# A hybrid decoder layer on one core: decay with a bias in the exponential, splits on VectorE, tables in pieces, and new planner costs

## The chip, the cores and the metric

The kernel runs on one core of a Trainium2 chip. The metric is the device time of one execution in microseconds (us). The engines are TensorE (PE; its weight loads are PEld), VectorE (DVE), ScalarE (ACT), GpSimd (POOL) and SyncE (SP), whose queue issues most of the DMAs. Each engine runs its own instructions in order and waits on semaphores for the others.

## What is computed

One decoder layer over 2048 tokens of width 1024, all in float32: a normalised input goes through one projection, three groups of heads read parts of it, their outputs are gated, projected and added to the input, and a last normalisation follows.

```python
h = rms_norm(x, norm_in)
c_q, c_kv, k_rope, gdn_qkv, gdn_a, gdn_b, mem_q, gate = split_cols(h @ w_in, IN_SPLITS)
...
qkv = silu(causal_depthwise_conv(gdn_qkv, gdn_conv))
gq, gk = l2_normalize(gq), l2_normalize(gk)
beta = sigmoid(gdn_b); g = -exp(a_log) * softplus(gdn_a + dt_bias)
...
g = cumsum(g, axis=-1)
decay = exp(where(incl, g[..., :, None] - g[..., None, :], -inf))
L = where(strict, einsum(k_beta, k) * decay, 0)
T = triangular_solve(L + eye, eye)
...
mixed = concatenate([o_mla, o_gdn, o_mem]) * silu(gate)
y = rms_norm(x + mixed @ w_out, norm_final)
```

The three groups have four heads each: causal attention with low-rank queries and keys and rotary positions (MLA), a gated delta rule (GDN), and attention over 256 memory tokens.

## The kernel before

**Stages.** The tokens are worked on in two halves of 1024, each as two blocks of 512. The input projection streams 34 column tiles of `w_in` (`stream`, `run_unit`) over the resident, transposed input. Beside it run, for each half, four GDN heads (`delta_head`), the two low-rank paths (`low_rank` with `q_use` and `kv_use`), and once the projection of the memory tokens (`mem_proj`). Then come the attention scores and values, and last the output projection with the final norm (`out_half`).

**Precision.** A float32 product is made of three passes of a faster type: an operand is split into a rounded part (`hh`, `wh`) and the rest (`hl`, `wl`), and `mm3` multiplies hi by hi, hi by lo and lo by hi into one PSUM tile (`ip` for the input projection). For every half tile of weights `w_split` makes `wh` (a copy, on ACT or DVE by `copy`) and `wl` (a subtraction, on POOL or DVE by `lesser`). `small_weights` does the same for the low-rank and memory weights (`bwh`, `bwl`).

**A GDN head.** After convolution and normalisation, `delta_head` loads rows of the cumulated decay to all partitions (`gr`), subtracts the column's own value (line 903), adds a mask (904), and takes the exponential on ACT (905). The score blocks (`kk`) times this decay give `LT`, which goes through DRAM (`lsys`, `lt`) to POOL. POOL solves 32x32 triangular systems in 62 small `TENSOR_TENSOR` instructions (`pr`, `X`; lines 949 to 955), and the result returns through DRAM (`tsys`) into `inv`. DVE transposes its blocks (`STREAM_TRANSPOSE mid<-inv`), PE joins them (`inv` matmuls), and a scan over eight chunks follows, in which each step waits for the one before: PE (`pa`), DVE (`r`), PE, ACT (`vn`), PE, DVE (the new state, `st` and `st_odd` in turn), PE. At every fourth chunk transposed values `vt` and keys `kt` are scaled from PSUM on DVE (line 1028).

**Rotary positions.** `trig_tables` writes sine and cosine to DRAM (`trig`). `key_rope` loads each table twice into 64 partitions, `q_use` four times into 128, by `trig_load`: one DMA whose source has a leading broadcast dimension of 2 or 4. `key_rope` runs four times and `q_use` loads four times, so there are eight `cs` and eight `sn` loads.

**What sets the order.** The program is written out by a planner in Python. It keeps a clock per engine (`T`), adds to it the cost of each instruction as it is recorded (`act_cost`, `dve_cost`, `pool_cost`, `pe_cost`), and lets the foreground (the projection, later attention) run until a background generator is due by that clock. A `yield n` in a generator says how many ns to wait after its last step. Several constants take part: `CBIAS` in `copy` chooses ACT or DVE, `SLACK` and the POOL clock in `lesser` choose POOL or DVE, `BACK` says how far ahead of PE's clock a DMA may be issued, `MEM_AT` after how many tiles of a half `mem_proj` starts. So every cost and constant moves the places of instructions on all engines. Nearly all instructions pass through one recording helper and carry its line, 259; they are told apart by their tiles.

Of the kernel before, what the change touches and what calls it, by code (L numbers as in the profile page):

```python
# [15 lines left out]
ALU = mybir.AluOpType  # L16
# [19 lines left out]
EARLY = 0.0  # L36
BACK = 2000.0
AVM = 600.0
SECOND = 2
TRIG_AT = 1  # L40
MEM_AT = 44
STRICT = False
SPARE = 500.0
LONG = "012k3q", "0123qk"
CONV = 4
CBIAS = 2000.0
DEFER = -1500.0
# [20 lines left out]
def hybrid_layer(ctx, tc, a, out):  # L68
# [154 lines left out]
    def pool_cost(op, args, kw, out):  # L223
        if op == "tensor_tensor":
            return 147 + 2.1 * free(out)
        fast = op == "tensor_scalar" and kw["op0"] == ALU.mult and kw.get("op1") == ALU.add
        return 160 + (0.85 if fast or op == "memset" else 3.4) * free(out)

    def pe_cost(op, args, kw, out):
        src = args[2] if op == "matmul" else args[1]  # L230
        if op == "transpose":
            return 109 if src.shape[0] > 32 else 53
        n, m, k = free(src), free(args[1]), src.shape[0]
        if src.dtype == F32:
            return 1.667 * max(n, m) + 4 if n >= 96 or k < P else 3.33 * max(n, m)
        return 0.4167 * n + 3

# [292 lines left out]
    def trig_load(t, i, c, n):  # L530

        dma(out=t[0:n * 32],
            in_=trig[i, c].unsqueeze(0).broadcast_to([n, 32, 512]))

# [79 lines left out]
    def w_split(w):  # L614
        wh = sb.tile([P, 512], F32R, name="wh", tag="wh", bufs=3)
        copy(wh, w)
        wl = sb.tile([P, 512], F32R, name="wl", tag="wl", bufs=3)
        lesser("wl").tensor_tensor(wl, w, wh, op=ALU.subtract)
        return wh, wl
# [131 lines left out]
    def token_scalars(hf, res):  # L751
# [6 lines left out]

        at, bt, z, z2, pl, gc = (tk(i) for i in range(6))
        dma(out=at, in_=ab[hf, 0:4].rearrange("h (c t) -> (h c) t", t=P))  # L760
        dma(out=bt, in_=ab[hf, 4:8].rearrange("h (c t) -> (h c) t", t=P))
        yield 3500

# [32 lines left out]
        V.scalar_tensor_tensor(ce, eg, -1.0, bt, op0=ALU.mult, op1=ALU.mult)  # L796
        V.tensor_scalar(hb, bt, 0.5, None, op0=ALU.mult)
        dma(out=rows_g[hf].rearrange("(r t) -> r t", t=P), in_=gc)
        dma(out=rows_l[hf].rearrange("(r t) -> r t", t=1), in_=eg[:, P - 1:P])
# [4 lines left out]
        pc = psg("pc")  # L804
        for i, t in enumerate((gc, hb, ce, rem, eg)):
            PE.transpose(pc[:, i * 32:(i + 1) * 32], t, ident[0:32, 0:32])
# [36 lines left out]
    def delta_head(hf, h, q, k, res):  # L843
# [53 lines left out]
        for b in range(2):  # L897
# [4 lines left out]
            gr3 = gr.rearrange("p (c t) -> p c t", t=P)  # L902
            V.tensor_tensor(gr3, gr3, gc.unsqueeze(2).broadcast_to([P, 4, P]), op=ALU.subtract)
            V.tensor_tensor(gr3, gr3, neg.unsqueeze(1).broadcast_to([P, 4, P]), op=ALU.add)
            A.activation(gr, gr, AF.Exp)
            k3, q3 = (t[:, bs].rearrange("p (c t) -> p c t", t=P) for t in (k, q))
# [111 lines left out]
        for c in range(NCK):  # L1018
            cl = h * 8 + c
            if c % 4 == 0:  # L1020
# [3 lines left out]
                for src, o, dst, col in ((v, 0, vt, cols[:, 1, cl:cl + 4]), (k, c, kt, kfac[:, 1, c:c + 4])):  # L1024
                    ps = psg("tr")
                    for cc in range(4):
                        PE.transpose(ps[:, cc * P:(cc + 1) * P], src[:, (o + cc) * P:(o + cc + 1) * P], ident)
                    V.tensor_tensor(dst, ps.rearrange("p (c t) -> p c t", t=P),
                                    col.unsqueeze(2).broadcast_to([P, 4, P]), op=ALU.mult)
                    yield 0  # L1030
# [61 lines left out]
    def small_weights(srcs):  # L1092
# [6 lines left out]
        def split(w):  # L1099
# [3 lines left out]
            wl = sb.tile([P, n], F32R, name="bwl", tag="m2", bufs=9)  # L1103
            lesser("bwl").tensor_tensor(wl, w, wh, op=ALU.subtract)
            return wh, wl
# [645 lines left out]
    def out_half(tb, n, ps, ss):  # L1751
# [4 lines left out]
        yield 0  # L1756
        A.activation(xo[:, 1, ns], xo[:, 0, ns], AF.Square, accum_out=ss[:, n:n + 1])
        if n == 0:
            return
# [4 lines left out]
        V.reciprocal(rs, rs)  # L1764
        yield 0
        for n in range(2):
            ns = slice(n * 512, (n + 1) * 512)
# [432 lines left out]
```

## Time and profile before

| | |
|---|---|
| median of three runs | 1797.79 us (1794.03 to 1803.4) |
| the profiled execution | 1803.16 us, its span 1801.3 us |
| PE busy | 1741.0 us, 97% of the span |
| DVE, ACT, POOL busy | 65%, 41%, 28% |
| mean granted TensorE clock | 0.987 |

The profile is of one execution. A row of the timeline has start and duration in us, engine, operation, the tiles written and read, shapes, and in brackets how long the engine was idle before it and what released it. In windows, "busy (x)" is busy time with the number of instructions, PEclk the granted TensorE clock as a share of full speed, DMA the mean busy share of the 16 DMA engines. A PE busy share near 100% says only that no gap is seen, since matmuls are pipelined; their number in a window tells the pace.

### The profile page before, as it was taken

To read this page: it belongs to the slowest core of one execution; us is meant where nothing else is said; L and a number is where in the kernel's file an instruction comes from. 1 tells how busy PE (TensorE), PEld (TensorE's weight loads), DVE (VectorE), ACT (ScalarE), POOL (GpSimd) and SP (SyncE) were. 2 spreads that over 40 slices of the span, in tenths; PEclk is the share of its full clock that TensorE was granted. 3 is DMA by queue.
4 is the path that set the end of the run, shared out by engine and by line. 5 is a ranking of instruction groups with operands and counts; after the bars stand their busy time and mean duration, and the time that the engine had idled before them with its cause. 6 is when DMAs were issued, how large, how long until landed. Compare 5 with 4: busy or idle time off the path is not lost.

```text
span 1801.3 us, 28573 instructions
## 1 busy us (share of the span) xinstructions
PE 1741.0 (97%) x9776; PEld 1466.0 (81%) x9776; DVE 1170.3 (65%) x2629; ACT 732.4 (41%) x1880; POOL 500.4 (28%) x891
## 2 busy tenths in 40 slices
PE   7999999999999999999999999999999999999998
PEld 6778787888877787887888787899999998888886
DVE  7877766776686847666556754777776777345343
ACT  7444233342453535253334432446465556212121
POOL 1421743351631124434432261001011012321120
PEclk9999999999999999999999998999999999999999
DMA  7544474436556343576633567835342536666551
GB/s 269 163 129 147 140 231 126 144 113 211 157 181 209 111 152 115 173 225 199 205 121 103 174 183 229 254 117 153 87 157 66 157 113 197 197 188 185 165 169 49
DMA packets 225826, 291.19 MB, mean 162 GB/s; under 512 B 30320, under 2 KB 130672, under 8 KB 225680
## 3 DMA queue, kind: packets, MB, share of 16 engines
q1 hardware_dynamic: 218640, 273.62, 48.8%
q0 software_dynamic: 7040, 15.74, 3.1%
q8 instruction: 77, 1.26, 0.3%
q14 instruction: 69, 0.57, 0.1%
HBM read 197.79 MB, written 91.49 MB: 161 GB/s over the span
## 4 chain that ended last, share of the span: by engine, by line
PE 45%; DMA 3%; DVE 2%; POOL 2%; issue 1%; ACT 0%; SPq 0%; DVEq 0%; POOLq 0%; ACTq 0%
PE op L259 15%; PE sc L259 10%; PE av L259 7%; PE ip L259 5%; PE pt L259 4%; PE pa L259 1%; POOL X L259 1%; PE qb L259 1%; POOL pr L259 1%; DMA sn<-trig 1%; PE mk L259 1%; PE mv L259 0%; PE inv L259 0%; SPq L305 0%; DMA og<-gatem 0%
## 5 line engine op out<-in xcount | busy, mean ns | idle before, releaser
L259 PE MATMUL ip<-hh,wh 128*128 128x512 f32 x1088 | 457.6, 421 | 10.8 <-ACT hh L259 8.2
L259 PE MATMUL ip<-hh,wl 128*128 128x512 f32 x1088 | 432.5, 398 | 4.9 <-DVE wl L259 4.1
L259 PE MATMUL ip<-hl,wh 128*128 128x512 f32 x1088 | 432.2, 397 | 0.0
L259 PEld LDWEIGHTS ip<-hh,wl 128*128 128x128 f32 x1088 | 207.3, 191 | 50.7 <-DVE wl L259 4.5
L259 PEld LDWEIGHTS ip<-hh,wh 128*128 128x128 f32 x1088 | 208.5, 192 | 47.2 <-ACT hh L259 8.2
L259 PEld LDWEIGHTS ip<-hl,wh 128*128 128x128 f32 x1088 | 208.7, 192 | 34.8 <-DVE hl L259 0.5
L259 POOL TENSOR_TENSOR wl<-wr,wh 128x512 fp32r<-128x512 f32 x73 | 105.8, 1449 | 408.3 <-ACT wh L259 357.4
L259 ACT CAST wh<-wr 128x512 fp32r<-128x512 f32 x143 | 88.5, 619 | 170.3 <-PE ip L259 115.3
L259 DVE TENSOR_TENSOR tl<-pt,th 128x512 fp32r<-128x512 f32 (+2 forms) x208 | 119.7, 584 | 28.0 <-ACT th L259 25.9
L259 DVE SCALAR_TENSOR_TENSOR y<-raw,gdn_conv,y 128x512 f32<-128x512 f32 x144 | 118.1, 824 | 23.0 <-ACT y L259 21.4
L259 PE MATMUL sc<-kn,qn 128*128 128x512 f32 (+2 forms) x480 | 132.7, 380 | 0.4 <-DMA qn<-qn 0.4
L259 PE MATMUL op<-wop,mh 128*128 128x512 f32 x416 | 130.8, 395 | 0.0
L259 PE MATMUL av<-th,vn 128*128 128x256 f32 x576 | 130.8, 288 | 0.0
L259 ACT CAST th<-pt 128x512 fp32r<-128x512 f32 (+2 forms) x157 | 80.3, 517 | 101.3 <-PE pt L259 92.0
L259 POOL TENSOR_TENSOR pr<-X,lt 128x60 f32<-128x60 f32 (+24 forms) x248 | 97.7, 394 | 58.9 <-DMA lt<-lsys 40.1
L294 POOL DMA_DIRECT2D mix<-mo x64 | 34.8, 544 | 263.4 <-ACT mo L259 179.7
L259 PEld LDWEIGHTS av<-th,vn 128*128 128x128 f32 x576 | 99.3, 190 | 4.7 <-ACT th L259 0.7
L259 POOL TENSOR_TENSOR X<-X,pr 128x60 f32<-128x60 f32 (+24 forms) x248 | 96.6, 390 | 19.4
L259 PE MATMUL sc<-kr,qr 128*128 128x512 f32 (+2 forms) x320 | 97.9, 383 | 0.0
L259 PEld LDWEIGHTS op<-wop,mh 128*128 128x128 f32 x416 | 77.4, 188 | 17.7
L259 ACT ACTIVATE s<-s,m 128x768 f32<-128x768 f32 (+13 forms) x71 | 79.1, 1115 | 30.3 <-DVE mx L259 30.3
L259 POOL TENSOR_TENSOR og<-og,orow 128x512 f32<-128x512 f32 x28 | 40.9, 1485 | 171.9 <-DMA orow<-ri 117.0
(285 smaller groups left out, 3581.9 us busy)
## 6 DMA issues: line engine op xcount, KB each, us to landing
wr<-in_w_in SPq DMA_DIRECT2D x148, 256.0 KB, 3.0
fr<-rows_n SPq DMA_DIRECT2D x48, 256.0 KB, 4.6
mxo<-mix SPq DMA_DIRECT2D x16, 768.0 KB, 5.4
craw<-craw SPq DMA_DIRECT2D x40, 256.0 KB, 2.8
x<-in_xT SPq DMA_DIRECT2D x32, 256.0 KB, 5.2
gatem<-gt SPq DMA_DIRECT2D x32, 256.0 KB, 2.9
qn<-qn SPq DMA_DIRECT2D x32, 256.0 KB, 3.3
kn<-kn SPq DMA_DIRECT2D x32, 256.0 KB, 3.0
```

The lines of the kernel that those rows point to most:

```text
L259: return pinned(f(*args, **kw))
L294: pinned(nc.gpsimd.dma_start(out=raw(out), in_=raw(in_)))
```

## The change

1. `token_scalars` also makes the negated cumulated decay `ngc`, and its column form takes the place of `gc` in `cols`. In `delta_head` the subtraction on DVE is gone; the exponential is four ACT instructions of 128 columns, each with its column of `ngc` as bias.
2. `kt` is written by four ACT instructions with the column factor as scale; `vt` stays on DVE.
3. `trig_load` issues one DMA per copy of the table, each into 32 partitions.
4. `wl` and `bwl` are always made on DVE.
5. For the last token block, `out_half` multiplies by the gain before the row's factor is known, scales the halves on ACT and DVE, and stores them in two DMAs.
6. The planner's costs and constants: a POOL `tensor_tensor` costs more (290 + 2.25 per column for 147 + 2.1), a matmul costs 5 ns more, `BACK` 4000 for 2000, `MEM_AT` 30 for 44, `CBIAS` 500 for 2000, and `token_scalars` waits 2000 for 3500.

```diff
-BACK = 2000.0
+BACK = 4000.0
-MEM_AT = 44
+MEM_AT = 30
-CBIAS = 2000.0
+CBIAS = 500.0
@@ pool_cost, pe_cost
-            return 147 + 2.1 * free(out)
+            return 290 + 2.25 * free(out)
-        return 0.4167 * n + 3
+        return 0.4167 * n + 8
@@ trig_load
-        dma(out=t[0:n * 32],
-            in_=trig[i, c].unsqueeze(0).broadcast_to([n, 32, 512]))
+        for j in range(n):
+            dma(out=t[j * 32:(j + 1) * 32], in_=trig[i, c])
@@ w_split (and bwl in small_weights)
-        lesser("wl").tensor_tensor(wl, w, wh, op=ALU.subtract)
+        V.tensor_tensor(wl, w, wh, op=ALU.subtract)
@@ token_scalars
-        yield 3500
+        yield 2000
+        V.tensor_scalar(ngc, gc, -1.0, None, op0=ALU.mult)
-        for i, t in enumerate((gc, hb, ce, rem, eg)):
+        for i, t in enumerate((ngc, hb, ce, rem, eg)):
@@ delta_head
-            V.tensor_tensor(gr3, gr3, gc.unsqueeze(2).broadcast_to([P, 4, P]), op=ALU.subtract)
             V.tensor_tensor(gr3, gr3, neg.unsqueeze(1).broadcast_to([P, 4, P]), op=ALU.add)
-            A.activation(gr, gr, AF.Exp)
+            for c in range(4):
+                A.activation(gr3[:, c, :], gr3[:, c, :], AF.Exp, bias=gc[:, c:c + 1])
-                    V.tensor_tensor(dst, ps.rearrange("p (c t) -> p c t", t=P),
-                                    col.unsqueeze(2).broadcast_to([P, 4, P]), op=ALU.mult)
+                    if dst is kt:
+                        for cc in range(4):
+                            A.activation(kt[:, cc, :], ps[:, cc * P:(cc + 1) * P], AF.Copy, scale=col[:, cc:cc + 1])
+                    else:
+                        V.tensor_tensor(dst, ps.rearrange("p (c t) -> p c t", t=P),
+                                        col.unsqueeze(2).broadcast_to([P, 4, P]), op=ALU.mult)
@@ out_half, last token block
+        ends = tb == out_order()[-1]
+        if ends:
+            V.tensor_tensor(xo[:, 0, ns], xo[:, 0, ns], gf[0][:, ns], op=ALU.mult)
...
+        if ends:
+            A.activation(xo[:, 0, 0:512], xo[:, 0, 0:512], AF.Copy, scale=rs)
+            dma(out=out[tb * P:(tb + 1) * P, 0:512], in_=xo[:, 0, 0:512])
+            V.tensor_scalar(xo[:, 0, 512:1024], xo[:, 0, 512:1024], rs, None, op0=ALU.mult)
+            dma(out=out[tb * P:(tb + 1) * P, 512:1024], in_=xo[:, 0, 512:1024])
+            give(hb=1)
+            return
```

By count, DVE gets 73 `wl` of the streamed weights that POOL had (75 become 148), 19 `bwl`, and 42 copies to `wh` and `bwh` that ACT had (`wh` 5 become 41); it loses 16 `gr` subtractions and 16 `kt`. POOL keeps the solves, the table arithmetic and the output stage. SP's queue gets 33 DMAs more.

**DVE at the second head's inversion** (`mid<-inv` are its block transposes, `st` and `st_odd` the first head's scan). Before:

```order
L259 SCALAR_TENSOR_TENSOR r<-pa,kfac,vt 128x128
L259 SCALAR_TENSOR_TENSOR y<-raw,gdn_conv,y 128x512
L259 SCALAR_TENSOR_TENSOR y<-raw,y 128x512
L259 TENSOR_TENSOR elo<-vb,ehi 128x512
L259 STREAM_TRANSPOSE mid<-inv_280 32x256 x2
L259 SCALAR_TENSOR_TENSOR st_odd<-st_253,el,pa 128x128
L259 SCALAR_TENSOR_TENSOR r<-pa,kfac,vt 128x128
```

and in the changed kernel:

```order
L259 TENSOR_TENSOR y<-y,fr 128x512
L259 TENSOR_TENSOR gr<-gr,norms 128x512
L259 SCALAR_TENSOR_TENSOR gt<-th,gt 128x512
L259 TENSOR_TENSOR wl<-wr,wh 128x512
L259 STREAM_TRANSPOSE mid<-inv_280 32x256
L259 SCALAR_TENSOR_TENSOR st_253<-st_odd,el,pa 128x128
L259 STREAM_TRANSPOSE mid<-inv_280 32x256
L259 TENSOR_TENSOR vt<-tr,cols 128x512
```

A state update still stands behind a transpose. On PE, the order puts 331 matmuls between this head's last `kk` and its first `inv` before, and 359 in the changed kernel.

**DVE at the third rotary table load of the queries** (`ra`, `rb`, `rc` read the tables `cs` and `sn`). Before:

```order
L259 SCALAR_TENSOR_TENSOR r<-pa,kfac,vt 128x128
L259 RECIPROCAL ri_259<-sm 128x1
L259 TENSOR_TENSOR ra<-qb,cs 128x512
L259 TENSOR_TENSOR rb<-qb,sn 128x512
L259 TENSOR_TENSOR rc<-qb,cs 128x512
L259 SCALAR_TENSOR_TENSOR st_odd<-st_256,el,pa 128x128
```

and in the changed kernel:

```order
L259 TENSOR_TENSOR ra<-qb,cs 128x512
L259 TENSOR_TENSOR rb<-qb,sn 128x512
L259 TENSOR_TENSOR rc<-qb,cs 128x512
L259 TENSOR_TENSOR vt<-tr,cols 128x512
L259 TENSOR_TENSOR cs<-qb,sn 128x512
L259 TENSOR_TENSOR ra<-ra,rb 128x512
L259 TENSOR_TENSOR rc<-rc,cs 128x512
L259 SCALAR_TENSOR_TENSOR r<-pa,kfac,vt 128x128
```

The rotation now stands ahead of the head's first scan step instead of inside it.

**DVE at the first head's decay** (`wl` needs the `wh` of its half tile). Before:

```order
L259 TENSOR_TENSOR gr<-gr,cols 128x512
L259 TENSOR_TENSOR sn<-ra,cs 64x512
L259 TENSOR_TENSOR gr<-gr,neg 128x512
L259 SCALAR_TENSOR_TENSOR y<-raw,gdn_conv,y 128x512
L259 TENSOR_TENSOR kq<-y,fr 128x4x128
L259 SCALAR_TENSOR_TENSOR y<-raw,gdn_conv,y 128x512
L259 TENSOR_TENSOR raw<-ip,rms 128x512
L259 TENSOR_TENSOR wl<-wr,wh 128x512
```

and in the changed kernel, behind the same decay rows:

```order
L259 TENSOR_TENSOR sn<-ra,cs 64x512
L259 SCALAR_TENSOR_TENSOR y<-raw,y 128x512
L259 TENSOR_TENSOR raw<-ip,rms 128x512
L259 CAST wh<-wr 128x512
L259 SCALAR_TENSOR_TENSOR y<-raw,gdn_conv,y 128x512
L259 TENSOR_TENSOR wl<-wr,wh 128x512
L259 SCALAR_TENSOR_TENSOR y<-raw,gdn_conv,y 128x512 x2
L259 TENSOR_TENSOR wl<-wr,wh 128x512
```

The subtraction `gr<-gr,cols` is gone; two splits now stand within seven rows of DVE's queue, one of them with its copy.

## Rows read from the trace of the kernel before

**Rows 1.** The page: busy time, share of the span and instructions of each engine.
```profile
PE 1741.0 (97%) x9776; PEld 1466.0 (81%) x9776; DVE 1170.3 (65%) x2629; ACT 732.4 (41%) x1880; POOL 500.4 (28%) x891
```

**Rows 2.** Windows of PE, output stage: window, PE busy (x), PEclk, DMA share, GB/s.
```profile
1575.00:1620.00 45.00, 45.00 (x198) 1.00 0.64 195
```

**Rows 3.** Windows, input stage: PE, PEld, DVE, ACT, POOL busy (x), PEclk, DMA, GB/s.
```profile
0.00:270.00 270.00, 249.05 (x1191) 202.11 (x1192) 197.24 (x405) 118.96 (x277) 103.40 (x171) 0.97 0.58 180
0.00:1110.00 1110.00, 1064.13 (x5795) 874.81 (x5796) 748.24 (x1526) 450.09 (x1210) 399.31 (x728) 0.98 0.54 168
```

**Rows 4.** Waits of PE: who waited for whom, us in total, times, longest.
```profile
PE pa L259 <- DVE st_odd L259: 12.6, 7, 3.5
...
PE ip L259 <- DVE wl L259: 4.1, 1, 4.1
...
PE pc L259 <- DVE tks L259: 2.4, 2, 2.3
...
PE inv L259 <- DVE mid L259: 1.0, 2, 0.6
```

**Rows 5.** Windows at PEclk 0.50; columns as in Rows 3.
```profile
71.90:75.30 3.40, 3.00 (x8) 2.30 (x8) 1.02 (x1) 0.67 (x3) 3.15 (x4) 0.50 1.26 70
133.40:140.10 6.70, 5.37 (x13) 4.21 (x14) 6.70 (x10) 2.06 (x4) 2.50 (x2) 0.50 0.25 78
286.90:290.30 3.40, 3.40 (x11) 2.72 (x10) 2.19 (x14) 0.62 (x4) 0.00 (x0) 0.50 0.22 77
590.80:594.10 3.30, 3.30 (x10) 2.53 (x9) 3.22 (x6) 0.71 (x2) 0.00 (x0) 0.50 0.29 102
1092.50:1099.30 6.80, 6.80 (x46) 5.12 (x46) 2.72 (x9) 2.34 (x7) 0.00 (x0) 0.50 0.50 163
1119.80:1123.20 3.40, 3.40 (x13) 2.99 (x13) 3.40 (x7) 1.57 (x4) 0.00 (x0) 0.50 0.35 128
```

**Rows 6.** Timeline of PE at the scan: start us, us, instruction, [idle before <-releaser].
```profile
285.86 0.49 PE L259 MATMUL pa<-st,y 128*128 128x128 f32 x2 [3.37 <-DVE st_odd L259]
...
589.66 0.49 PE L259 MATMUL pa<-st,y 128*128 128x128 f32 x2 [2.80 <-DVE st_odd L259]
...
1119.52 0.59 PE L259 MATMUL pa<-st,y 128*128 128x128 f32 x2 [3.50 <-DVE st_odd L259]
```

**Rows 7.** Timeline of DVE near 284 us.
```profile
283.80 0.43 DVE L259 STREAM_TRANSPOSE mid<-inv 32x256 f32<-32x256 f32 x1 [4.74 <-DMA inv<-tsys]
...
285.46 0.35 DVE L259 SCALAR_TENSOR_TENSOR st_odd<-st,el,pa 128x128 f32<-128x128 f32 x1
```

**Rows 8.** Timeline of DVE and of SP's queue at the rotary tables.
```profile
581.57 1.39 DVE L259 TENSOR_TENSOR rb<-kr,sn 32x512 f32<-32x512 f32 x2 [1.68 <-DMA sn<-trig]
...
1106.98 0.53 SPq L305 DMA_DIRECT2D sn<-trig  x1
...
1117.93 0.69 DVE L259 TENSOR_TENSOR rb<-qb,sn 128x512 f32<-128x512 f32 x1 [4.16 <-DMA sn<-trig]
```

**Rows 9.** Window just after two table loads; columns as in Rows 3.
```profile
97.50:101.00 3.50, 3.50 (x19) 2.89 (x18) 1.89 (x3) 2.77 (x12) 1.29 (x1) 1.00 0.15 51
```

**Rows 10.** Timeline of ACT and of DVE, one pair wh and wl.
```profile
129.12 0.62 ACT L259 CAST wh<-wr 128x512 fp32r<-128x512 f32 x1
...
133.53 1.15 DVE L259 TENSOR_TENSOR wl<-wr,wh 128x512 fp32r<-128x512 f32 x1
```

**Rows 11.** Groups: line engine op, shapes xcount | busy us, mean ns | idle before, releaser.
```profile
L259 POOL TENSOR_TENSOR wl<-wr,wh 128x512 fp32r<-128x512 f32 x73 | 105.8, 1449 | 408.3 <-ACT wh L259 357.4
...
L259 DVE SCALAR_TENSOR_TENSOR y<-raw,gdn_conv,y 128x512 f32<-128x512 f32 x144 | 118.1, 824 | 23.0 <-ACT y L259 21.4
...
L259 DVE TENSOR_TENSOR wl<-wr,wh 128x512 fp32r<-128x512 f32 x75 | 53.5, 714 | 28.1 <-ACT wh L259 24.7 <-POOL bwl L259 2.6 <-PE tr L259 0.4
...
L259 DVE SCALAR_TENSOR_TENSOR xo<-xo,rs,gf 128x512 f32<-128x512 f32 x32 | 22.6, 748 | 0.5
...
L259 ACT ACTIVATE sq<-sq 128x128 f32<-128x128 f32 x128 | 33.9, 265 | 4.2 <-PE sq L259 2.0
```

More of the change, by code (lines that the diff above doesn't have):

```diff
@@ L757, in tk @@
             return pg[0:32, i * P:(i + 1) * P]
-        at, bt, z, z2, pl, gc = (tk(i) for i in range(6))
+        at, bt, z, z2, pl, gc, ngc = (tk(i) for i in range(7))
         dma(out=at, in_=ab[hf, 0:4].rearrange("h (c t) -> (h c) t", t=P))
         dma(out=bt, in_=ab[hf, 4:8].rearrange("h (c t) -> (h c) t", t=P))
-        yield 3500
+        yield 2000
         V.tensor_scalar(bt, bt, -1.0, 80.0, op0=ALU.mult, op1=ALU.min)
@@ L1103, in split @@
             wl = sb.tile([P, n], F32R, name="bwl", tag="m2", bufs=9)
-            lesser("bwl").tensor_tensor(wl, w, wh, op=ALU.subtract)
+            V.tensor_tensor(wl, w, wh, op=ALU.subtract)
             return wh, wl
```

## The prediction

> **What bounds it now.** I read the page first, then windows, PE's waits and the timeline at the longest of them. PE is busy for 97% of the span [rows 1], and in the output stage 198 matmuls of 512 columns pass in 45 us, 0.227 us each, with no gap [rows 2]. The change leaves the matmuls as they are, so it can only win what PE loses: 60 us of the span in which PE is not busy (1801.3 - 1741.0), and the time at the lower clock. The input stage holds most of it, 46 us in the first 1110 [rows 3]. No other engine is full there, but DVE comes nearest: 748 of 1110 us, and 197 of the first 270 (73%) [rows 3].
>
> The list of PE's waits shows who is late: DVE with the scan's state (12.6 us in 7 waits), with one `wl` (4.1), with the token scalars `tks` (2.4), with `mid` (1.0) [rows 4]. Each of these stalls has a second price. Within a few us of it PE's granted clock stands at 0.50 (1.2 instead of 2.4 GHz) for 3.3 to 6.8 us [rows 5], with PE at work nearly throughout, so each such stretch loses half its length again: 1.7 or 3.4 us.
>
> **The inversion's place.** At 283.80 DVE stood idle for 4.74 us at a block transpose, because the solve's result was still on its way, and the first head's state update behind it came only at 285.46 [rows 7]; PE waited 3.37 us for that [rows 6], and the clock was down from 286.9 to 290.3 [rows 5]. The last head shows the same: PE waits 1.0 us for `mid` [rows 4] ahead of the stretch from 1092.5. The new POOL cost prices the 62 small instructions of a solve some 150 ns higher each, so the planner puts the transposes later. The order shows it: counted at 0.227 us per 512 columns, the matmuls between a head's last `kk` and its first `inv` were worth 53 to 64 us in the eight heads, and are now worth 63 to 70. Some 9 us more than before cover the 4.74 us. Gain: 3.4 + 1.7 for the second head, 1.0 + 3.4 for the last, 9.5 us. If the cover is gone, the state update still stands behind a transpose and the stall comes back whole.
>
> **The table loads.** At 1106.98 SP issued `sn`, and DVE could go on with `rb` only at 1117.93, 11 us later, 4.16 of them idle; near 581 it lost 1.68 at another `sn` [rows 8]. State updates stood behind both, and PE waited 3.50 and 2.80 us [rows 6], with clock stretches at 1119.8 and 590.8 [rows 5]. The row that explains it is the quiet window after two loads of two copies each: the DMA engines are busy to a share of 0.15 and move 51 GB/s [rows 9], about 2.4 of 16 engines. So a table in one DMA runs on few engines, and in pieces of 32 partitions it should use more. I take the whole of the later stall (3.5 + 1.7) and of the earlier one the part that was idle for `sn` (1.7) with its clock (1.65): 8.5 us. The pieces put 32 more DMAs into SP's queue, at about the 0.53 us of an issue [rows 8], in groups of four or eight. Behind them stand weight loads, which are asked for two half tiles ahead; no wait of PE in the list goes back to them, so I add nothing, and at most one such group, 8 x 0.53 = 4 us.
> The Trainium skill (DMA: Bandwidth & Descriptors, Rules for kernel authors) says that a leading broadcast dimension of c copies keeps a DMA on at most c engines; the trace agrees with its 0.15. The same table of rules advises against two transfers to separate partition ranges, since both use the same engines one after the other. By that rule alone the pieces would win nothing and the sum would be 8.5 us smaller; the row of 0.15 speaks against it here, and it stays as a rival below.
>
> **The token scalars.** PE waited 2.4 us for `tks` [rows 4], with the clock stretch from 71.9 [rows 5]. The first of these transposes had 50 us of matmuls ahead of it in the order, and has 57 now. Gain 2.3 + 1.7 = 4.0 us.
>
> **The splits on DVE.** What goes to DVE: 73 `wl` at 0.71 us [rows 11], 19 `bwl` and 42 copies of the same size at about 0.7, 95 us. What leaves it: 32 passes over 128x512, at the same 0.7, 22 us. And POOL's reads slow DVE where both inputs are in SBUF: the convolution step takes 824 ns in the mean while the same form in the output stage takes 748 [rows 11], 76 ns x 144 = 11 us for this group alone. So DVE gets about 60 us more in 1110, from 67% to 73%. POOL's 1449 ns per `wl` [rows 11] is replaced by DVE's 714 plus its queue, and the queue is what counts: the one `wl` that PE waited for was DVE's, its `wh` done at 129.74 and the subtraction begun at 133.53, eight DVE instructions later [rows 10]. Price of such a stall: 4.1, and 3.4 for its clock [rows 5]. It came once among 75 on DVE; 73 more make 7.5 us at most by that rate, and nothing if DVE gains what POOL gives back. I take the middle, 3.7, and leave the old one where it is. At the opening one `wl` more stands ahead of the block's first evacuation: 0.7 us.
>
> **Edits at nothing.** Decay: DVE's pass is counted above; ACT gets 64 short instructions for 16 long ones and 64 for `kt`, some 0.27 us each [rows 11], and gives up 42 copies; it is at 41% [rows 1]. If ACT were late, the next score block would be, and PE has projection work between. `ngc` is two small DVE instructions. The tail: two passes of 0.75 [rows 11] become one on each of two engines, but the new multiplication by the gain waits for the square and stands ahead of the factor; gain and loss are one pass each, 0 within 1. Earlier `mem_proj` and `BACK` move work that PE does anyway.
>
> **Sum.** -9.5 - 8.5 - 4.0 + 3.7 + 0.7 = -17.6 us. Against the profiled execution (1803.2 us, span 1801.3) that is 1785.6. That execution lies 5.4 us above the median of the runs shown; against the median, 1797.8, it is **1780 us**.
>
> **Rivals.** (a) *The stalls only change places.* All places behind the first 130 us are dealt anew, and the planner does not see the clock. For it: the named stalls come from an order chosen by the same planner. Against it: three causes have lost their mechanism. Time 1798, within 9.
> (b) *DVE becomes the bound of the first stage* and PE waits for splits, as at 134 us. For it: DVE is at 73% in the first 270 us and the splits come on top; two `wl` now stand within seven rows. Against it: the split needs DVE 0.7 us per half tile, which PE takes 2.7 us or 5.4 us to use. Each such stall costs 7.5. The gains less the opening are 21.3 us, so three more stalls make it even and four put it 9 us behind; with five it is 1797.8 - 21.3 + 37.5 = 1814 us.
> (c) *The pieces don't help*, because they queue on the same engines (the Trainium skill's advice above): 8.5 us less gain, 1789 us, no change.
> (d) *More is won*: the stall at 134 us goes as well (7.5) and the splits cost nothing (3.7): 1769 us; at 1757, 41 of PE's 60 us would be gone.
>
> **Chances.** Of no change a measurement of this kernel can tell about 0.5%, 9 us. My forecast has 0.53 and lies under 1788.8; (d) 0.10; together faster 0.63. (a) 0.12 and (c) 0.10: same 0.22. (b) 0.15: slower. The range runs from 1757, the far end of (d), to 1804, through (c) and most of (a); beyond it lie (b) and a little at either end.
>
> **What would show it.** Right: no idle time of DVE for `tsys` ahead of a transpose or for `trig`; a DMA share well above 0.15 behind the table loads; no stretch at 0.50 behind a table load or a transpose, where five of the six of [rows 5] lie or follow `tks`; the convolution step at about 750 ns. Wrong: PE's list headed by `ip <- DVE wl` or `ip <- DVE wh`, or new waits of DVE on PE's path with new stretches at 0.50 behind them.

## The result, and the profile after

The changed kernel takes 1779.78 us (median of four runs, 1773.92 to 1787.0), the kernel before beside it 1799.84 (four runs). The ratio is 0.990, with a 95% interval of 0.9877 to 0.9923: 18 us less, 20 by the medians. The prediction was 1780 us, 17.6 us less. The profiled execution took 1773.92 us, 5.9 under its median; that of before lay 3.3 over its own. So 9 of the 29.2 us between the two spans are the choice of executions.

The page, to be held against [rows 1]:

```profile
PE 1723.1 (97%) x9776; PEld 1455.7 (82%) x9776; DVE 1180.8 (67%) x2726; ACT 742.2 (42%) x1956; POOL 376.0 (21%) x799
```

PE has the same 9776 matmuls and 18 us less busy time, and the span is 1772.1 us. Two losses explain nearly all of it. PE is not busy for 49.0 us (1772.1 - 1723.1), where it was 60.3: 11.3 less. And the mean granted clock is 0.996 for 0.987: (1 - clock) x span gives 7.1 us for 23.4, 16.3 less. Together 27.6 of the 29.2 us.

The clock's part of this is a matter of the two executions, though. The mean clock differs between executions of one kernel: over the four of the changed kernel it lies between 0.991 and 0.996, a loss of 7 to 16 us, 11.6 in the mean. For the kernel before, the profile's 0.987 is the only value of this comparison; in the 47 executions of it beside the experiments it lies between 0.987 and 0.994, a loss of 15.6 us in the mean. By these means the clock gives about 4 us and not 16. What is left of the spans without it is steadier: 1765 to 1769 us in the four, 1775.5 in the mean of the 47 and 1777.9 in the profile of before, so 9 to 11 us less, as much as PE's idle time says.

Windows of after: the two of [rows 3], the one that stands behind table loads as in [rows 9], and the two stretches at half clock that are left with PE at work, where [rows 5] lists six.

```profile
0.00:270.00 270.00, 251.24 (x1232) 205.25 (x1233) 208.31 (x456) 122.51 (x316) 68.20 (x142) 0.99 0.59 182
0.00:1110.00 1110.00, 1075.94 (x5949) 889.50 (x5950) 777.35 (x1692) 463.97 (x1301) 276.28 (x639) 1.00 0.56 175
97.50:101.00 3.50, 3.50 (x17) 2.92 (x16) 1.36 (x3) 1.67 (x10) 0.00 (x0) 1.00 0.81 255
106.00:112.80 6.80, 5.19 (x13) 4.15 (x14) 1.71 (x9) 0.00 (x0) 0.00 (x0) 0.50 0.50 134
1495.20:1498.70 3.50, 2.99 (x13) 2.80 (x13) 2.54 (x3) 2.45 (x7) 3.37 (x5) 0.51 1.18 309
```

The trace of before has three more stretches at half clock than [rows 5] lists, 17 us long together. They lie behind waits of PE for `abt` (2.5 us), `acc` (3.8), and `th` and `tl` (1.8 and 1.1):

```profile
37.90:41.30 3.40, 3.40 (x10) 2.68 (x9) 2.93 (x6) 3.40 (x7) 1.28 (x1) 0.52 0.89 264
689.90:696.70 6.80, 5.28 (x15) 4.36 (x16) 5.70 (x19) 1.23 (x3) 0.00 (x0) 0.51 0.36 83
1512.50:1519.30 6.80, 6.12 (x29) 6.15 (x30) 5.02 (x11) 2.87 (x8) 1.27 (x3) 0.51 0.79 230
```

In the first 1110 us PE is idle for 34 us, where it was 46. DVE is at 70% there (777 us; the prediction said 73) and POOL lost 123 us. In the window behind the table loads the DMA engines are at 0.81 and move 255 GB/s, where it was 0.15 and 51; but x1 below shows nearly the same there with whole tables.

PE's waits, to be held against [rows 4] (who waited for whom: us in total, times, longest), and the one wait of DVE for a table that is left, out of 10.7 us in five waits of before (9.4 for `sn`, 1.3 for `cs`):

```profile
PE pa L259 <- DVE st_odd L259: 7.0, 6, 1.8
PE rn L259 <- DVE fac L259: 3.9, 1, 3.9
PE ip L259 <- DVE wl L259: 3.0, 3, 1.6
...
PE inv L259 <- ACT mid L259: 0.2, 1, 0.2
...
DVE ra L259 <- DMA cs<-trig: 2.1, 1, 2.1
```

`st_odd` fell from 12.6 to 7.0 us and its longest wait from 3.5 to 1.8. `tks` and DVE's `mid` are gone from the list, and DVE has no idle time for `tsys` (6.8 us before). New is the wait for `fac`, the factors of the first head, at 104 us: DVE waited 2.1 us for `cs` just ahead of them, and the stretch at 0.50 from 106.0 follows.

Groups (xcount | busy us, mean ns | idle before), the answers to [rows 11] and the two new forms on ACT:

```profile
L259 DVE TENSOR_TENSOR wl<-wr,wh 128x512 fp32r<-128x512 f32 x148 | 103.3, 699 | 45.0 <-ACT wh L259 40.6 <-PE pa L259 1.5 <-PE ip L259 0.5
...
L259 DVE SCALAR_TENSOR_TENSOR y<-raw,gdn_conv,y 128x512 f32<-128x512 f32 x144 | 109.1, 763 | 19.1 <-ACT y L259 17.7
...
L259 ACT ACTIVATE gr<-gr,cols 128x128 f32<-128x128 f32 x64 | 21.0, 393 | 26.8 <-DVE gr L259 26.7
...
L259 ACT ACTIVATE kt<-tr,kfac 128x128 f32<-128x128 f32 x64 | 18.3, 370 | 21.1 <-PE tr L259 21.0
```

The convolution step is at 763 ns, from 824. The page shows DVE with 97 instructions more and only 10.5 us more busy time (1180.8 for 1170.3).

### The profile page after: what moved, and what is told of

It is laid out like the page before. It is cut to its first block, busy times and chain, and to the rows that moved or that the text cites. A ratio compares the mean times of both kernels' runs of the same rounds, so it can differ in the third digit from the quotient of the medians.

```text
span 1772.1 us, 28706 instructions
## 1 busy us (share of the span) xinstructions
PE 1723.1 (97%) x9776; PEld 1455.7 (82%) x9776; DVE 1180.8 (67%) x2726; ACT 742.2 (42%) x1956; POOL 376.0 (21%) x799
## 4 chain that ended last, share of the span: by engine, by line
PE 83%; DVE 8%; DMA 5%; ACT 3%; issue 1%; SPq 0%; POOL 0%; ACTq 0%; DVEq 0%
PE ip L259 34%; PE op L259 15%; PE sc L259 10%; PE av L259 6%; PE pa L259 4%; PE pt L259 4%; PE qb L259 3%; DVE y L259 1%; PE inv L259 1%; PE kk L259 1%; PE vb L259 1%; PE kb L259 1%; PE sq L259 1%; DMA bw<-in_w_mv 1%; PE tr L259 1%
## 5 line engine op out<-in xcount | busy, mean ns | idle before, releaser
L259 PE MATMUL op<-wop,mh 128*128 128x512 f32 x448 | 139.6, 392 | 0.0
L294 POOL DMA_DIRECT2D lt<-lsys x32 | 16.6, 525 | 550.4 <-DMA lsys<-LT 266.0
L259 DVE TENSOR_TENSOR wl<-wr,wh 128x512 fp32r<-128x512 f32 x148 | 103.3, 699 | 45.0 <-ACT wh L259 40.6
L259 DVE SCALAR_TENSOR_TENSOR y<-raw,gdn_conv,y 128x512 f32<-128x512 f32 x144 | 109.1, 763 | 19.1 <-ACT y L259 17.7
L259 ACT CAST wh<-wr 128x512 fp32r<-128x512 f32 x107 | 66.4, 621 | 102.4 <-PE ip L259 88.1
L259 PEld LDWEIGHTS op<-wop,mh 128*128 128x128 f32 x448 | 83.6, 188 | 18.6
L259 ACT ACTIVATE s<-s,m 128x640 f32<-128x640 f32 (+13 forms) x70 | 78.9, 1128 | 24.1 <-DVE mx L259 23.8
```

Source lines behind the costliest of these rows:

```text
L259: return pinned(f(*args, **kw))
L294: pinned(nc.gpsimd.dma_start(out=raw(out), in_=raw(in_)))
```

## The experiments

Twelve kernels ran, in three groups of four, each group on one chip with the kernel before between them (its medians there: 1792.2, 1792.7 and 1793.1 us). The ratio is to that kernel. The last two columns are the two losses as above, from each run's profiled execution (the clock is given to 0.001, so the last is good to 0.9 us). What is left of the span without them lies between 1711 and 1723 us in all fourteen profiles. Both columns are of one execution each, and the clock of one kernel moves by up to 0.007 from execution to execution, some 12 us in the last column.

| run | median us | ratio (95%) | PE not busy | (1 - clock) x span |
|---|---|---|---|---|
| before | 1799.8 | 1 | 60.3 | 23.4 |
| the change | 1779.8 | 0.9900 (0.9877 to 0.9923) | 49.0 | 7.1 |
| x1 one table DMA | 1792.8 | 1.0003 (0.9982 to 1.0023) | 64.5 | 14.3 |
| x2 old POOL price | 1773.7 | 0.9905 (0.9873 to 0.9937) | 51.9 | 10.7 |
| x3 splits by planner | 1810.1 | 1.0106 (1.0072 to 1.0140) | 68.6 | 23.5 |
| x4 matmul price 9 | 1771.9 | 0.9885 (0.9857 to 0.9913) | 45.6 | 7.1 |
| x5 before, pieces | 1789.5 | 0.9982 (0.9963 to 1.0000) | 55.4 | 14.3 |
| x6 before, splits on DVE | 1799.5 | 1.0037 (1.0018 to 1.0057) | 62.2 | 16.2 |
| x7 before, prices | 1804.8 | 1.0070 (1.0045 to 1.0095) | 66.1 | 25.2 |
| x8 decay on DVE | 1796.6 | 1.0018 (1.0002 to 1.0034) | 60.6 | 21.6 |
| x9 same, order kept | 1779.1 | 0.9926 (0.9911 to 0.9940) | 50.8 | 10.7 |
| x10 splits on POOL, order kept | 1805.1 | 1.0068 (1.0044 to 1.0092) | 73.1 | 14.4 |
| x11 before, matmul price 4 | 1811.6 | 1.0102 (1.0080 to 1.0124) | 68.6 | 14.4 |
| x12 key rotation later | 1773.9 | 0.9899 (0.9874 to 0.9925) | 42.4 | 5.3 |

The changed kernel itself was run only in the first comparison, where the kernel before took 7 us more than in the three groups. Prices against the changed kernel are differences of ratios here. By the bare medians x1 costs 13 us instead of 18, x3 30 instead of 37, x8 17 instead of 21, x9 nothing instead of 5 and x10 25 instead of 30, and x2, x4 and x12 are 6 to 8 us faster than the change.

Every edit to this program moves its whole order, so an edit's price and the price of the order that comes with it have to be told apart. Two means serve here: controls that move the order alone (x4, x11), and kernels that undo an edit while the planner is charged as if it had not been undone, so that the order stays (x1, x9, x10; x5 does the same from the other side).

**x1.** The queue gets the table whole, with the last of its pieces:

```diff
 def issue(t, out, in_, behind, awaited):
+    w = onedma.get(out.tensor.name)
+    if w:
+        w[0] -= 1
+        if w[0]:
+            return
+        _, out, in_ = onedma.pop(out.tensor.name)
     ins = pinned(nc.sync.dma_start(out=raw(out), in_=raw(in_)))
```

> The changed kernel with each rotary table fetched again by one DMA with a leading broadcast dimension; the planner is still charged for the pieces, so that the order of the work stays nearly the same. Theory (the pieces bring a table sooner): DVE sits idle for trig again, by 2 to 4 us in each of two or three places, and the time rises by the 8.5 us of the prediction, to about 1788 us (ratio to the kernel before 0.994). Rival 1 (the pieces queue on the same engines and win nothing): 1780 us, no idle time for trig. Rival 2 (in the new order the tables have more time ahead of them, so that even a slow load is hidden): DVE's idle time for trig stays under 3 us and the time is 1780 to 1783 us.

The gain was lost: 1.0003 against 0.9900, 18 us (13 to 24, from the two intervals). DVE's idle time for `trig` came back to 12.8 us in five waits. Timeline of x1 at two places (DVE, then ACT and PE; idle time and its releaser in brackets):

```profile
103.86 0.68 DVE L259 TENSOR_TENSOR ra<-kr,cs 32x512 f32<-32x512 f32 x1 [5.57 <-DMA cs<-trig]
...
106.39 0.68 DVE L259 TENSOR_TENSOR rb<-kr,sn 32x512 f32<-32x512 f32 x1 [1.85 <-DMA sn<-trig]
...
562.97 0.62 ACT L259 CAST wh<-wr 128x512 fp32r<-128x512 f32 x1 [8.36 <-DMA wr<-in_w_in]
...
563.64 0.80 PE L259 MATMUL ip<-hh,wh 128*128 128x512 f32 x1 [5.88 <-ACT wh L259]
```

and a window of it at the second (PE, PEld, DVE, ACT, POOL busy, PEclk, DMA, GB/s):

```profile
559.00:562.90 3.90, 0.00 (x0) 0.00 (x0) 0.00 (x0) 0.00 (x0) 0.00 (x0) 0.67 0.26 92
```

The two rows of DVE hold up `fac`: PE waits for it 9.07 us at 113.33, 3.86 in the changed kernel. The others are a second way to lose. SP had issued two whole tables at 552.5 and 553.1 and two loads of `wr` behind them, at 553.7. The weights landed 9 us later, and from 559 to 562.9 none of the five engines has anything to do, while the DMA engines are at 0.26. In the changed kernel the eight pieces are issued in 3.7 us, two loads of `wr` behind them; loads of `wr` there land after 2.9 to 4.2 us, and PE waits for no `wh`. The theory holds in kind; the forecast size was half.

The window that the prediction named does not tell pieces from whole tables. In x1 it is as full as in the changed kernel, because transfers of `craw` and a load of `wr` run in it as well; the DMA engines are quiet only later, while DVE still waits for `cs`:

```profile
97.50:101.00 3.50, 3.50 (x17) 2.89 (x16) 0.69 (x1) 2.09 (x13) 0.00 (x0) 1.00 0.80 245
102.00:104.00 2.00, 2.00 (x10) 1.52 (x9) 0.14 (x1) 0.00 (x0) 0.00 (x0) 1.00 0.13 49
```

The time from issue to use does tell them apart: this `cs` was issued at 97.34 and used at 103.86, 6.5 us later; in the changed kernel its pieces were issued from 96.86 and used at 99.93, 3.1 us later. DVE was idle for it in both.

**x2.** `return 290 + 2.25 * free(out)` becomes `return 147 + 2.1 * free(out)` in `pool_cost`.

> The changed kernel with the old planner price of POOL's tensor_tensor (147 + 2.1 per column), nothing else. Theory (the price puts the inversion's transposes behind its loads): the matmuls between the last kk and the first inv of a head fall back from 63 to 70 us to under 64, DVE sits idle at a transpose until tsys lands for some us, PE waits for st_odd by 3 us or more at once with a stretch at 0.50 behind it, and the time is about 1789 us (the prediction's 9.5 us less). Rival (the place of the solve did not matter, the order is only dealt anew): no idle time for tsys, 1775 to 1785 us.

No loss: 0.9905. Yet the mechanism is there, in full. By PE's rows the time from a head's last `kk` to its first `inv` was 64 to 74 us in the changed kernel, and is 56 to 65 here. Timeline of x2 near 900 us, DVE twice and PE:

```profile
899.77 0.43 DVE L259 STREAM_TRANSPOSE mid<-inv 32x256 f32<-32x256 f32 x1 [5.65 <-DMA inv<-tsys]
...
902.04 0.34 DVE L259 SCALAR_TENSOR_TENSOR st<-st_odd,el,pa 128x128 f32<-128x128 f32 x1
...
902.43 0.80 PE L259 MATMUL pa<-st_odd,y 128*128 128x128 f32 x2 [5.76 <-DVE st L259]
```

and its window at half clock behind that:

```profile
898.60:905.40 6.80, 2.97 (x10) 2.68 (x11) 3.60 (x8) 0.80 (x2) 2.31 (x5) 0.50 0.18 39
```

DVE sits idle for the solve's result, a state update stands behind the transpose, PE waits 5.76 us, and 6.8 us pass at half clock: 9.2 us, as the prediction had priced it (9.5 for two heads). But this order is without the wait for `fac` at 104 us and the stretch behind it (3.9 + 3.4 us). One stall more, one less.

**x3.** `wl` and `bwl` go through `lesser(...)` again.

> The changed kernel with wl and bwl again on POOL or DVE, as the planner chooses. Theory of the prediction (splits on DVE cost 3.7 us by waits of PE): 1776 us. Rival (POOL's reads slow DVE, which then is late for PE): the convolution step is back at about 824 ns from 763, DVE's busy time for the same work rises, PE waits longer for DVE and the time is 1785 to 1790 us. Third (the two cancel, or both lie beside other work): 1780 us within 3.

1.0106, 37 us over the changed kernel and more than the rival expected, though the convolution step went only to 777 ns. The largest single loss is a chain through five engines. Timeline of x3, POOL, SP's queue twice, DVE, ACT twice, PE:

```profile
485.58 1.09 POOL L259 TENSOR_TENSOR bwl<-bw,bwh 128x384 fp32r<-128x384 f32 x1
...
486.70 0.33 SPq L305 DMA_DIRECT2D bw<-in_w_q_b  x1
...
487.60 0.38 SPq L305 DMA_DIRECT2D gatem<-gt  x1
...
490.97 0.69 DVE L259 TENSOR_TENSOR gt<-ip,rms 128x512 f32<-128x512 f32 x1 [9.22 <-DMA gatem<-gt]
...
491.76 0.63 ACT L259 ACTIVATE th<-gt 128x512 f32<-128x512 f32 x1 [10.73 <-DVE gt L259]
...
492.76 0.27 ACT L259 COPY vn<-pa 128x128 f32<-128x128 f32 x1
...
493.08 0.80 PE L259 MATMUL pa<-vn,kt 128*128 128x128 f32 x2 [7.62 <-ACT vn L259]
```

and its window at half clock from there on:

```profile
487.90:498.20 10.30, 5.12 (x15) 4.25 (x16) 6.04 (x10) 4.01 (x8) 2.55 (x5) 0.50 0.45 141
```

Read the timeline from the bottom: PE waits 7.62 us for `vn`, which stands on ACT behind a `th` that waited 10.73 us for DVE's `gt`, which waited 9.22 us for `gatem`. SP issued that load only at 487.60, because ahead of it a load of `bw` needed a buffer which POOL's `bwl` was still to read. That subtraction had its `bwh` at 470.3, but stood on POOL behind the rest of a solve and the issue of its results, until 485.58. SP's queue was held for 17.0 us. Then 10.3 us at half clock: 7.6 + 5.2 = 12.8 us from one subtraction that was late on an engine for which PE itself waits 1.1 us in the whole run.

**x4.** `0.4167 * n + 8` becomes `+ 9` in `pe_cost`.

> The changed kernel with 9 instead of 8 ns in the planner's price of a matmul: no instruction changes, only the order is dealt anew from the first tiles on. It is the control for every other run. Theory (the gain belongs to mechanisms, not to one lucky order): 1780 us within 5, no idle time of DVE for tsys, under 3 us for trig. Rival (the gain is that of one order): 1788 to 1800 us, with new stalls of 3 us and stretches at 0.50 in other places.

0.9885, inside the interval of the changed kernel. The gain belongs to no single order. The stall for `fac` and the stretch behind it are there again.

**x5.** In the kernel before, `issue` sends a table as two or four DMAs of 32 partitions and charges one.

```diff
+    if in_.tensor.name == trig.tensor.name and out.shape[0] in (64, 128) and len(in_.shape) == 3:
+        for j in range(out.shape[0] // 32):
+            pinned(nc.sync.dma_start(out=raw(out[j * 32:(j + 1) * 32]), in_=raw(in_[j])))
+        return
```

> The kernel before with each rotary table in pieces of 32 partitions; the planner is charged for one DMA as before, so that the order stays nearly that of before. Theory (a table in one DMA is slow and holds DVE and what is queued behind it): DVE's idle time for trig falls from 10.7 us to under 2, the waits for st_odd of 2.8 and 3.5 us near 590 and 1119 us go, and the time falls by 8.5 us (the prediction) to 13 us (what the opposite edit cost in the changed kernel): 1779 to 1784 us, ratio 0.993 to 0.995. Rival (the pieces help only in the new order): 1788 to 1792 us.

DVE's idle time for `trig` is gone (none for 10.7 us) and PE's waits for `st` and `st_odd` fell from 16.1 to 8.9 us, as the theory said. But the time fell by 3 us only (0.9982, 0.9963 to 1.0000), as the rival said. Its profile has 14 us less of the two losses than that of before, but that one is from the first comparison, 10 us above the medians here. In the old order the pieces are worth 0 to 7 us.

**x6.** In the kernel before, `wl` and `bwl` always on `V`.

> The kernel before with wl and bwl always on DVE, the planner free to deal the order anew. Theory from the opposite edit (splits on POOL hold weight buffers behind a solve, and POOL's reads slow DVE): the convolution step falls from 824 to about 765 ns, and the time falls by 10 to 30 us, to 1762 to 1782 us. Rival 1 (rival b of the prediction, DVE becomes late for PE): PE's list is headed by wl, 1795 to 1814 us. Rival 2 (the 30 us of the opposite edit were one bad order): 1788 to 1796 us.

1.0037: slower by 7 us, against the theory. PE waits for `wl` (8.3 us in three waits) and for `fac` (7.6), and behind the second stands a table, for which DVE sat idle 6.55 us. Waits of DVE in x6, 15.6 us for tables:

```profile
DVE rb L259 <- DMA sn<-trig: 8.5, 5, 3.3
...
DVE ra L259 <- DMA cs<-trig: 7.1, 2, 6.6
```

The convolution step fell from 824 to 749 ns, as expected: without POOL's subtractions DVE is faster. That the splits alone run into tables which the pieces would have brought in time fits these waits, but the two together were not run, and the order is a new one too, which alone can move the time by more than 7 us (x11).

**x7.** The kernel before with the six new prices and constants and nothing else.

> The kernel before with the planner's new prices and constants alone (POOL 290 + 2.25, a matmul +5 ns, BACK 4000, MEM_AT 30, CBIAS 500, the token scalars' 2000). Theory after the run with the old POOL price, which lost nothing: the prices deal the order anew and win nothing by themselves, 1785 to 1799 us. Rival (the prediction's inversion place and token scalars): 13.5 us less, about 1779 us, no idle time for tsys and no wait for tks.

1.0070, 12 us slower. The waits that the prediction wanted gone are gone: DVE has no idle time for `tsys`, PE none for `tks`. Others took their places: `st_odd` 9.1 us in six waits, the longest 3.7; `vn` 4.8; `kr` 3.9; `y` 3.8.

**x8.** Subtraction and `kt` on DVE again (as an addition of the negated column), one exponential.

```diff
-            for c in range(4):
-                A.activation(gr3[:, c, :], gr3[:, c, :], AF.Exp, bias=gc[:, c:c + 1])
+            V.tensor_tensor(gr3, gr3, gc.unsqueeze(2).broadcast_to([P, 4, P]), op=ALU.add)
+            A.activation(gr, gr, AF.Exp)
-                    if dst is kt:
+                    if False:
```

> The changed kernel with the decay's subtraction again on DVE (as an addition of the negated column) and one exponential of 512 columns, and kt scaled on DVE: 32 passes of 0.7 us go back to DVE, 128 short ACT instructions become 16 long ones. Theory (the prediction's edits at nothing): the 22 us of DVE lie beside other work, 1775 to 1783 us. Rival (DVE is the engine that PE waits for, so what it sheds counts): PE waits longer for DVE, 1785 to 1795 us.

1.0018, 21 us slower than the changed kernel, as the rival said. But the largest loss is not DVE's work. Timeline of x8, DVE and PE:

```profile
1083.10 0.43 DVE L259 STREAM_TRANSPOSE mid<-inv 32x256 f32<-32x256 f32 x1 [8.34 <-DMA inv<-tsys]
...
1083.68 0.28 PE L259 MATMUL inv<-mid,LT 32*32 32x32 f32 x2 [6.99 <-DVE mid L259]
```

and its window at half clock around that:

```profile
1081.40:1091.70 10.30, 7.33 (x76) 5.77 (x77) 5.39 (x15) 1.96 (x5) 3.10 (x8) 0.50 0.30 87
```

DVE was idle, for the solve of the last head, whose first `inv` came 50 us after its last `kk` (64 in the changed kernel). That is an order, so it was run again with the order kept.

**x9.** The edit of x8, but ACT is charged for four exponentials and four `kt`, and DVE for neither of its two passes.

> The changed kernel with decay and kt on DVE as in the run before, but the planner is charged as if nothing had been undone, so that the order stays that of the changed kernel. It tells the price of DVE's 22 us by itself from the price of another order. Theory (the edit is worth about nothing, and the 20 us of the run before were another order with a stall at the last head's inversion): 1775 to 1783 us, no wait of PE for mid above 1 us. Rival (DVE's time itself counts): 1790 us or more again, with more waits for st, st_odd, fac and wl.

0.9926: 5 us slower than the changed kernel (0 to 9), with 50.8 us of PE's idle time for 49.0, and no wait for DVE's `mid`. So of x8's 21 us about 5 are the edit and about 17 the order.

**x10.** As x9, for the splits: the planner is charged for DVE, and POOL does 82 `wl` and 12 `bwl`.

```diff
+    def split_on(name, wl, w, wh):
+        note("DVE", dve_cost("tensor_tensor", (wl, w, wh), {}, wl), [wl], [w, wh])
+        if max(T["POOL"], pool_at[0], solving[0]) <= T["PE"] + SLACK[name]:
+            pool_at[0] = max(T["POOL"], pool_at[0], T["PE"]) + 147 + 2.1 * free(wl)
+            pinned(nc.gpsimd.tensor_tensor(wl, w, wh, op=ALU.subtract))
+        else:
+            pinned(nc.vector.tensor_tensor(wl, w, wh, op=ALU.subtract))
```

> The changed kernel with 82 wl and 12 bwl on POOL (the kernel before has 74 and 19), while the planner is charged as if they were on DVE: the order stays nearly that of the changed kernel. Theory (POOL's reads slow DVE, and a weight buffer that POOL frees behind a solve holds SP's queue): the convolution step is back above 800 ns, SP's queue is held by POOL's wl for over 10 us at a time, and the time is 1790 to 1810 us. Rival (the loss of the earlier run came from its other order): 1775 to 1785 us.

1.0068 against 0.9900: 30 us (24 to 36), in nearly the same order. So the splits' place is the largest part of the change, in this order, which was dealt for splits on DVE. The page of x10:

```profile
PE 1732.1 (96%) x9776; PEld 1459.6 (81%) x9776; DVE 1172.8 (65%) x2633; ACT 740.0 (41%) x1956; POOL 509.7 (28%) x892
```

its waits of PE:

```profile
PE pa L259 <- DVE st_odd L259: 9.7, 7, 2.8
PE ip L259 <- POOL wl L634: 9.1, 5, 5.0
...
PE rn L259 <- DVE fac L259: 5.5, 1, 5.5
PE pa L259 <- DVE st L259: 4.8, 7, 1.5
```

and one of its groups:

```profile
L259 DVE SCALAR_TENSOR_TENSOR y<-raw,gdn_conv,y 128x512 f32<-128x512 f32 x144 | 113.9, 798 | 21.9 <-ACT y L259 20.6
```

DVE has 93 instructions less than in the changed kernel, some 64 us of work at 0.69, and is busy for only 8.0 us less (1172.8 for 1180.8): POOL's reads take back 56 us of what POOL takes over. The rest of DVE's work is later by that much, and the waits for `st_odd`, `st` and `fac` grow from 12.5 to 20.0 us in sum (the changed kernel has 1.6 for `st`). The convolution step was expected above 800 ns and is at 798. SP's queue was held by POOL's `wl` for 9.5 us at most, not over 10; the changed kernel's longest hold, by DVE's `wl`, is no shorter. Waits of SP's queue, x10 and then the changed kernel:

```profile
SPq L305 <- POOL wl L634: 149.7, 52, 9.5
...
SPq L305 <- DVE wl L259: 213.2, 79, 10.0
```

With DVE's `wl` the sum for x10 is 269 us, 55 more than in the changed kernel and 10 less than before, but no wait of PE is shown to come from it. What the list does show at PE is its own wait for POOL's `wl`, 9.1 us, and the 7.5 us more for `st_odd`, `st` and `fac`: 16.6 of the 24.1 us by which PE is idle longer than in the changed kernel.

**x11.** In the kernel before, `0.4167 * n + 3` becomes `+ 4`.

> The kernel before with 4 instead of 3 ns in the planner's price of a matmul: the control on the other side, no instruction changes. Theory (a new order moves the time of the kernel before by about as much as the three single parts did): somewhere between 1785 and 1805 us. Rival (an order is worth little): within 3 us of before, 1790 to 1796 us, and the single parts' losses are their own.

1.0102: 18 us for another order of the same work. It falls on the very mechanisms of the prediction. Waits of DVE in x11:

```profile
DVE rb L259 <- DMA sn<-trig: 10.2, 5, 3.0
...
DVE mid L259 <- DMA inv<-tsys: 8.7, 6, 4.7
```

and behind them PE waits 22 us for `st_odd` and `st`.

**x12.** As x4, and `key_rope` yields 4000 for 2000 behind its loads.

> The changed kernel with 9 ns in the planner's price of a matmul, and the key rotation asked for 4000 instead of 2000 ns after its loads: the first head's norms and factors come ahead of it on DVE. A try to beat both kernels. Theory: PE's wait of 3.9 us for fac near 104 us and the stretch at 0.50 behind it go, 6 to 7 us, from 1772 to about 1766 us (ratio 0.985). Rival (the new order brings a stall elsewhere): 1772 to 1785 us.

The wait at 104 us and its stretch are gone, and PE's idle time (42.4 us) and the clock's loss (5.3) are the lowest of all. The time is not: 0.9899, inside the interval of the changed kernel. Neither x4 nor x12 can be told from it.

## Why the prediction was right, and where its steps were not

**Right: what bounds it, and what a stall costs.** The gain is PE's idle time (11.3 us) and the clock behind it (16.3 in the profiled pair, about 4 in the mean of the executions). Of the clock the prediction priced five of the six stretches of [rows 5], 10 us, and left out the three that it did not list, 8.5 us. In all fourteen profiles the span without these two is the same within 6 us either way.

**Wrong: the splits on DVE, +3.7.** The sign and the size. With the order kept they are worth 30 us (x10). The prediction had both facts and weighed them singly: POOL's reads slow DVE, and PE waits for DVE. It took 11 us for the first, from one group, and so 60 us more work for DVE in the first 1110 us; it became 29 (777 for 748), and in x10 POOL's reads take back 56 of 64 us. It did not ask what PE would wait for POOL's own `wl` in the new order (9.1 us in x10), nor that `wl` and `bwl` free the buffers on which SP's queue waits, behind POOL's solves; that this reaches PE is shown at one place (x3).

**Right in kind, too small: the table loads, -8.5.** DVE's waits for `trig` fell from 10.7 to 2.1 us, and undoing it costs 18 us in the new order (x1). The missing part is one that the prediction did not price: weight loads that stand behind a whole table, 6 us of PE's time and the clock. It only asked whether the pieces would delay them. Its sign for the pieces, a DMA share well above 0.15, proves nothing, as x1 has 0.80 in that window with whole tables. In the old order the pieces won 3 us alone (x5), so the size hangs on what stands behind the loads.
The Trainium skill (DMA: Bandwidth & Descriptors, Rules for kernel authors) advises against separate transfers to separate partition ranges. With this source, a broadcast, the trace disagrees: 3.1 us from issue to use in pieces, 6.5 us whole, and 18 us of the whole time (x1); its other rule, on the leading broadcast dimension, is the one that decides here.

**Right in kind, wrong as a sum: the inversion's place (-9.5) and the token scalars (-4.0).** The new prices do remove both waits (x7), and the old POOL price brings one back at the predicted price (x2). But x7 is 12 us slower and x2 no slower: a new order brings other stalls. The step that failed is to count the stalls that a new order takes away and none that it brings.

**Edits at nothing.** The decay is worth 5 us (0 to 9; x9), so nothing was nearly right. ACT's new instructions take 393 and 370 ns, not 0.27 us; the row taken was one without a column operand. ACT is at 42%, and no wait of PE in the changed kernel names either of them. The tail stands: from the end of the last matmul to the end of the span 7.2 us before and 7.4 now. The opening's 0.7 us did not come: PE's wait for `abt` near 36 us is 2.0 us, from 2.5.

**So the sum was right by balance.** In the changed kernel's own order the splits, the pieces and the decay are worth 30, 18 and 5 us, 53 in all (38 by the bare medians), and the gain is 18 to 20. The parts don't add: alone they gave +7 (x6) and -3 us (x5), and the prices +12 (x7). What fits all runs, though it is only argued, is that the order of before was a good one for its work. Two other orders of the same work, x7 and x11, lie 0.7 and 1.0% above it; four orders of the new work (the change, x2, x4, x12) lie together between 0.9885 and 0.9905. Between the means of the three and the four lie 1.6%, 29 us. On this reading the order of before avoided many places where a late table or a late split could hurt; the change takes these causes away, so that most orders are good. Not all: x8 shows one that loses 17 us.

**The rivals.** (a), that the stalls only change places, is half of the truth: another order alone moved the time by 17 or 18 us (x11; x8 against x9), twice the 9 us given to it. (b), that DVE becomes the bound, is what x6 may show a little of, and only without the pieces. (c), that the pieces win nothing, falls with x1. (d), that more is won, came true by half: the stall at 134 us is gone (the longest wait for `wl` is 1.6 us, with no stretch behind it), which the sum had left in with 7.5 us. The new wait for `fac` and its stretch, 3.9 + 3.4 us, take that back.

**What stays open.** Whether the old work has orders as good as the new, since only three were run; and why x12 is no faster with the smallest losses. Part of that is the choice of execution: the profiled one had the highest clock of its four (0.997; the others 0.992 to 0.996).

## What to carry to other kernels

Before an edit to a program whose order a planner deals, run two or three neutral changes of a price: here they moved the time by up to 1%, as much as the edit. To price an edit, undo it with the order kept. Read the clock's share from several executions: here it moved by 9 to 13 us between executions of one kernel. And an engine that PE hardly waits for still has a price in three places: the access to SBUF that it shares, the buffers it frees, and the queue that waits for these.

## What the runs showed of the hardware

POOL and DVE slow each other, and not evenly. The tile `wl` in x10 (shortest, median and longest of its instructions on POOL, ns):

```profile
L634 POOL TENSOR_TENSOR wl<-wr,wh x81: 1261/1292/6764, 32.3 to 1089.0; 128x512 fp32r<-128x512 f32 x81
```

The same subtraction takes 1.29 us in the median and up to 6.76. Timeline of DVE and PE around the longest:

```profile
137.21 2.72 DVE L259 SCALAR_TENSOR_TENSOR y<-raw,gdn_conv,y 128x512 f32<-128x512 f32 x4
139.86 0.67 DVE L259 TENSOR_TENSOR y<-y,fr 128x512 f32<-128x512 f32 x1
...
141.66 1.40 DVE L259 SCALAR_TENSOR_TENSOR y<-raw,gdn_conv,y 128x512 f32<-128x512 f32 x2
...
144.24 0.77 PE L259 MATMUL ip<-hh,wl 128*128 128x512 f32 x1 [4.97 <-POOL wl L634]
```

and its window there (PE, PEld, DVE, ACT, POOL busy):

```profile
137.20:143.20 6.00, 2.07 (x10) 1.37 (x8) 5.86 (x10) 1.12 (x3) 5.78 (x1) 1.00 0.14 50
```

DVE runs instructions with two inputs in SBUF back to back, from 137.21 to 143.06. POOL is busy with one subtraction for 5.78 of these 6 us, ends it 1.1 us after DVE's chain, and PE waits 4.97 us for it. In the other direction DVE's convolution steps grow from 763 to 798 ns in the mean, and in the kernel before they fall from 824 to 749 when the subtractions leave POOL (x6). The Trainium skill (GPSIMD Engine Reference, Key points) says that POOL shares its SBUF interfaces with VectorE and that the contention comes with DVE instructions of two SBUF inputs, among others. The trace agrees, and under this chain of them POOL hardly moved.

A table in one DMA holds up the loads issued behind it: in x1 `wr` landed 9 us after its issue, with the DMA engines at 0.26 at the end; behind the pieces of the changed kernel it took 2.9 to 4.2 us.
